# A two-layer fp32 encoder on one Trainium2 core: inner results of w_down's seven-product pairs added to X by adding DMAs, one such pair also in layer 0's last chunk, layer 1's attention steps sooner

## The chip, the cores and the metric

The kernel runs on one core of one Trainium2 chip. The metric is the device time of one execution in microseconds (us); lower is better. The median of three runs of the kernel before is 2045.56 us (2045.43 to 2046.12). One execution was profiled, and every time below that is not a run's time is read from that execution.

## The reference, cut to what matters

Sequence 256, model width 2048, two layers, everything in fp32. Layer 0 mixes tokens with a gated MLP, layer 1 with grouped-query attention (12 query heads, 4 key heads, head width 128, per-head norms and a rotary table). Both layers also attend into 256 memory tokens, and both end in a SwiGLU feed-forward part of width 5632.

```python
def gqa_axial_attention(qkv, g_q, g_k, cos, sin):
    ...
    def block(qi):
        s = jnp.einsum('bqhgd,bkhd->bhgqk', qi, k).astype(jnp.float32) * scale
        p = jax.nn.softmax(s, axis=-1).astype(v.dtype)
        return jnp.einsum('bhgqk,bkhd->bqhgd', p, v)
...
def swiglu(h, w_gate_up, w_down):
    gate, up = jnp.split(h @ w_gate_up, 2, axis=-1)
    return (jax.nn.silu(gate) * up) @ w_down
...
    for l in range(DEPTH):
        ...
        x = x + jnp.concatenate([tok_out, mem_out], axis=-1) @ w_out[l]
        x = x + swiglu(rms_norm(x, g_ffn[l]), w_gate_up[l], w_down[l])
```

## The kernel before

**Numbers.** Every fp32 operand is split into a high part (`whi`, a cast on ScalarE, L254) and a remainder (`wlo`, a subtraction on VectorE, L255), and each product is three TensorE matmuls (L198 to L200: high by high, low by high, high by low). X, the running sum of the layers, lies in SBUF as tiles `x_t_j`: t is one of two halves of 128 tokens, j one of four blocks of 512 columns.

**The feed-forward part.** The 5632 features are cut into eleven blocks of 512 and those into three chunks: blocks 0 to 3, 4 to 7 and 8 to 10. For each chunk a `Pair` per block makes gate and up, and then two `Pair`s (jj = 0 and 1) multiply by w_down, each for two of the four column blocks of X, and add into X. A `Pair` goes through pairs of 128 rows of the weight. A pair of rows that is listed as quick takes the step `seven`: seven products of sums instead of eight plain ones, 21 matmuls instead of 24, for which VectorE first makes sums of weights (L347 to L350, into the tile `T`, split like the others: `wlo<-T`) and sums of activations. The other rows take the step `eight`. Four PSUM banks named `m` collect the inner products of the quick steps, and four named `acc` the outer products and all of the plain steps.

After a Pair's last quick step `inner()` reads the `m` banks: ScalarE copies one to a tile e (L397), and VectorE makes v, f, v again and y from the others (L398 to L401). Where the Pair adds into X, the four tiles e, f, v and y are then added to their X tiles by four VectorE instructions (L405), put off by 1 to 4 ticks through `later`. The four tiles have one buffer each. After the Pair's last plain step `outer(t)` adds the `acc` banks to the same X tiles (L413), which sets those banks free for the next Pair.

In w_down the quick rows are two per Pair in chunks 0 and 1 of both layers and one in the last chunk of layer 1; the last chunk of layer 0 has none.

**Attention in layer 1.** For each of three groups of four heads (c = 0, 1, 2) a `linear` makes the queries and `attend` queues seven steps with `later`, by a clock that `linear` moves on once for each 12 matmuls and a Pair a few times for each step: `queries` turns them (heads_T), `scores` multiplies two heads by the keys and starts the softmax (on VectorE a maximum, L481, a reciprocal, L488, and a scaling, L490; on ScalarE the exponentials, L485), `turn` turns the probabilities by TensorE (L500), `weigh` multiplies by the values. `scores`, `turn` and `weigh` come twice, for two heads each, one tick apart. After the third group three more linears follow: the queries of the memory attention, and the keys and the values made of the memory. `head_norm` normalises such keys and queries straight from the `acc` banks (on VectorE in L431), which sets the banks free. With four `acc` banks, two for each linear, the values' linear can't begin before the norm of the memory's queries has been made.

**What sets the order.** The order in which the program is written out gives priorities, and a scheduler that simulates the engines' times then fixes the order of the instructions on each engine. On the chip each engine takes its instructions strictly in that order. The weights come by DMAs that SyncE issues into four `raw` buffers; `whi` and `wlo` have three buffers each. GpSimd's queue (POOL) issues few DMAs: tables, and the memory's rows (L551).

Of the kernel before, what the change touches and what calls it, by code (L numbers as in the profile page):

```python
# [13 lines left out]
ALU = mybir.AluOpType  # L14
# [39 lines left out]
def encoder(ctx: ExitStack, tc: tile.TileContext, x, mem, g_mix, g_ffn, w_in_a, g_v_a, w_spatial, b_spatial,  # L54
            w_in_b, g_q_b, g_k_b, g_mem, w_mem_kv, g_mq, g_mk, w_out, w_gate_up, w_down, rope_c, rope_s, out):
    nc = tc.nc
# [14 lines left out]
    def nm(s):  # L71
        uid[0] += 1
        return f"{s}_{uid[0]}"

    def big(dt=F32, shape=None):
        return room["p"].tile(shape or [P, NB], dt, tag="a", name=nm("a"))
# [4 lines left out]
    def misc():  # L81
        return psm.tile([P, NB], F32, tag="m", name=nm("m"))

    def v4(a):
        return a.rearrange("p (c n) -> p c n", n=P)
# [10 lines left out]
    def later(delay, fn):  # L96
        queue.append((clock[0] + delay, len(queue), fn))
# [39 lines left out]
    def gslice(kind, l):  # L137
        return gcol[kind][:, 16 * l:16 * l + 16]
# [7 lines left out]
    ghead, rope_t = {}, {}  # L146
# [41 lines left out]
    def split(src, shape):  # L188

        hi = big(F32R, shape)  # L190
        lo = big(F32R, shape)
        nc.scalar.copy(hi, src)  # L192
        nc.vector.tensor_tensor(lo, src, hi.bitcast(F32), ALU.subtract)  # L193
        return hi, lo
# [7 lines left out]
    def transpose4(src, dst):  # L202
        for c in range(4):
            nc.tensor.transpose(dst[:, c * P:(c + 1) * P], src[:, c * P:(c + 1) * P], ident)  # L204
# [85 lines left out]
    def linear(parts, w, n0, units=kd, nk=KD):  # L290
        return Linear(parts, w, n0, nk).run(units)
# [18 lines left out]
    class Pair:  # L310
# [82 lines left out]
        def inner(self):  # L393

            b, o = self.bank, self.into
            e, v, f, y = [room["p"].tile([P, NB], F32, tag=f"e{i}", name=nm("e"), bufs=1) for i in range(4)]
            nc.scalar.copy(e, b[1])  # L397
            nc.vector.tensor_tensor(v, b[6], e, ALU.subtract)  # L398
            nc.vector.tensor_tensor(f, b[5], v, ALU.add)
            nc.vector.tensor_tensor(v, b[7], v, ALU.add)  # L400
            nc.vector.tensor_tensor(y, b[7], f, ALU.add)  # L401
            if o:
                for (t, n), x, op in (((0, 0), e, ALU.add), ((0, 1), f, ALU.add), ((1, 0), v, ALU.subtract),
                                      ((1, 1), y, ALU.add)):
                    later(1 + 2 * t + n, lambda o=o[t][n], x=x, op=op: nc.vector.tensor_tensor(o, o, x, op))  # L405
            self.out = o or [[e, f], [v, y]]

        def outer(self, t):
# [190 lines left out]
    def residual_turns(j, norm, g, parts):  # L599
        add_residual(None, j, norm, g, parts)  # L600
# [3 lines left out]
    norm = Norm()  # L604
    for l in range(DEPTH):
# [4 lines left out]
        if l == 0:  # L610
            w = w_in_a[0]
            v = [[None] * 3 for _ in range(NT)]
# [72 lines left out]
            acc = lin.acc  # L685
# [4 lines left out]
            for c in range(3):  # L690
                if c:
                    acc = linear(hT, w, TOK + c * NB)
# [11 lines left out]
            for c in range(3):  # L704
                acc = linear(hT, w, c * NB)
# [5 lines left out]
        else:  # L711
            w = w_in_b[0]
            own = {}
            load_tables(1)
            m.prep(20, 2)
            acc = linear(hT, w, TOK)
# [6 lines left out]
            own["v"] = scaled(linear(hT, w, TOK + MEMW), norm.r)  # L723
            for c in range(3):
                acc = linear(hT, w, c * NB)
                attend(head_norm(acc, norm.r, ghead["q"], True), (7, 8, 11, 13), lambda: own["k"], lambda: own["v"],
                       lambda h, c=c: (4 * c + h) // 3, 4 * c, cat)
            m.attend(linear(hT, w, TOK + 2 * MEMW), norm.r, cat)
            m.keys()
# [3 lines left out]
        norm = Norm()  # L733
# [25 lines left out]
        next_norm = Norm()  # L759
        for chunk in (range(0, 4), range(4, 8), range(8, 11)):  # L760
            aT, aS, half = Parts(), {}, {}
            quick = [2 * f + 1 for f in chunk[:2 if chunk[-1] < 10 else l]]

            def turn_a(a, t, f, aT=aT, aS=aS, half=half, quick=quick):
                tp = misc()
                transpose4(a, tp)
                hi, lo = split(v4(tp), [P, 4, P])
                for i in range(4):
                    aT.put(4 * f + i, t, hi[:, i, :], lo[:, i, :])
                i = 2 * f + 1  # L770
                if i in quick:
                    half[i, t] = big(F32, [P, 2, P])
                    nc.scalar.copy(half[i, t], v4(tp)[:, 2:4])
                    if t == NT - 1:
                        aS[i] = activation_sums(half[i, 0], half[i, 1])

            pairs = {}
            for f in chunk:
                order, some = ((3, 4, 5, 0, 6, 1, 7, 2), 2) if f == 0 else ((0, 3, 1, 4, 2, 5, 6, 7), 3)
                pairs[f] = Pair(hF, sums, w_gate_up[l], f * NB, DFF + f * NB, order, fast[:some])  # L780
            for f, g in pairs.items():
                g.run(pairs.get(f + 1))
                for t in range(NT):
                    a = kp.tile([P, NB], F32, tag="sg", name=nm("sg"), bufs=2)
                    nc.scalar.activation(a, g.out[t][0], AF.Silu, scale=norm.r[t])
                    nc.vector.scalar_tensor_tensor(a, g.out[t][1], norm.r[t], a, ALU.mult, ALU.mult)
                    later(3 + t if f == chunk[-1] else 12 + t, lambda a=a, t=t, f=f: turn_a(a, t, f))
            last = chunk[-1] == 10
            every = [2 * f + c for f in chunk for c in range(2)]
            slow = [i for i in every if i not in quick]  # L790
            pairs = []
            for jj in range(2):
                order = list(slow)
                for n, i in enumerate(quick):
                    order.insert(2 * n + (0 if jj and not last else 2), i)
                into = [[X[t][2 * jj + n] for n in range(2)] for t in range(NT)]
                pairs.append(Pair(aT, aS, w_down[l], 2 * jj * NB, (2 * jj + 1) * NB, order, quick, into))
            for jj, g in enumerate(pairs):
                g.run(None if jj else pairs[1])
                for j in (2 * jj, 2 * jj + 1):  # L800
                    if last and l < DEPTH - 1:
                        residual_turns(j, next_norm, gslice("mix", l + 1), hT)
                    elif last:
                        for t in range(NT):
                            parts = 2 if j == 3 and t == NT - 1 else 1
                            for i in range(parts):
                                cs = slice(i * NB // parts, (i + 1) * NB // parts)
                                eng = nc.scalar if i else nc.sync
                                eng.dma_start(out[0, t * P:(t + 1) * P, j * NB + cs.start:j * NB + cs.stop],
                                              X[t][j][:, cs])  # L810
        norm = next_norm
# [36 lines left out]
```

## Time and profile before

| | before |
|---|---|
| median of three runs | 2045.56 us |
| profiled execution | 2045.77 us |
| its span in the profile | 2044.0 us |
| mean granted TensorE clock | 0.999 |
| TensorE matmul (PE) busy | 2028.7 us, 99% |
| VectorE (DVE) busy | 1604.7 us, 79% |
| ScalarE (ACT) busy | 1095.1 us, 54% |
| GpSimd (POOL) busy | 49.1 us, 2% |
| DMA queues of SyncE, share of 16 engines | 56.4% |

The span runs from the first to the last instruction that the profile shows; the profiled execution took 1.77 us more than it. A busy share is an average over the whole span. Matmuls are pipelined, so the times of single matmuls in the rows overlap, and the pitch from start to start is what one costs.

### The profile page before, as it was taken

What the parts mean: (1) busy time and instruction counts of PE and PEld (TensorE: products, weight loads), DVE (VectorE), ACT (ScalarE), POOL (GpSimd) and SP (SyncE); (2) the same over time, 40 slices, a digit from 0 to 9 for tenths busy, and PEclk for the clock granted to TensorE, in tenths of its full rate; (3) what the DMA queues carried; (4) which work ended last, traced back from release to release, by engine and by line L of the source; (5) the groups of instructions that cost most, each with busy time, mean ns of one, the idle gap of its engine ahead of it and who ended that gap; (6) DMA issues with size and microseconds to landing.
All of it is one profiled execution on the core that took longest, in us unless ns stands there. A gap on an engine that the chain in (4) does not pass through costs nothing.

```text
span 2044.0 us, 24691 instructions
## 1 busy us (share of the span) xinstructions
PE 2028.7 (99%) x9298; PEld 1679.5 (82%) x9298; DVE 1604.7 (79%) x1862; ACT 1095.1 (54%) x1389; POOL 49.1 (2%) x80
## 2 busy tenths in 40 slices
PE   8999999999999999999999999999999999999999
PEld 6888888888888888888888888888888888888887
DVE  5575557998888988887666876589979899798976
ACT  7765455455444554445556665555544455444552
POOL 2010000000000000000010100000000000000000
PEclk9999999999999999999999999999999999999999
DMA  9754554655656556566556434655666555665554
GB/s 330 249 177 159 187 187 148 227 168 203 208 190 220 169 201 208 200 215 209 188 190 212 157 124 142 206 179 172 205 206 211 200 176 195 206 216 196 181 197 138
DMA packets 202432, 396.08 MB, mean 194 GB/s; under 512 B 11068, under 2 KB 11432, under 8 KB 202312
## 3 DMA queue, kind: packets, MB, share of 16 engines
q1 hardware_dynamic: 198800, 385.79, 56.4%
q0 software_dynamic: 2048, 6.42, 1.0%
q10 hardware_dynamic: 1464, 2.28, 0.3%
q8 instruction: 73, 1.20, 0.2%
q14 instruction: 47, 0.39, 0.1%
HBM read 390.26 MB, written 4.19 MB: 193 GB/s over the span
## 4 chain that ended last, share of the span: by engine, by line
PE 94%; DVE 3%; DMA 1%; issue 1%; ACT 1%; SPq 0%; DVEq 0%; ACTq 0%
PE acc L200 27%; PE acc L198 27%; PE acc L199 27%; PE m L200 4%; PE m L198 4%; PE m L199 4%; PE m L204 2%; DVE wlo L255 1%; DMA raw<-in_w_gate_up 1%; ACT whi L254 0%; PE m L500 0%; DMA x<-in_x 0%; DMA raw<-in_w_down 0%; PE m L643 0%; DVE x L413 0%
## 5 line engine op out<-in xcount | busy, mean ns | idle before, releaser
L255 DVE TENSOR_TENSOR wlo<-raw,whi 128x2048 fp32r<-128x2048 f32 (+2 forms) x465 | 836.4, 1822 | 227.0 <-ACT whi L254 224.8
L254 ACT CAST whi<-raw 128x2048 fp32r<-128x2048 f32 (+2 forms) x465 | 700.9, 1539 | 584.6 <-PE acc L199 513.3
L198 PE MATMUL acc<-whi,h 128*128 128x512 f32 x1440 | 563.6, 392 | 0.8 <-ACT whi L254 0.8
L199 PE MATMUL acc<-whi,h 128*128 128x512 f32 x1440 | 562.6, 391 | 0.0
L200 PE MATMUL acc<-wlo,h 128*128 128x512 f32 x1440 | 523.8, 392 | 1.1 <-DVE wlo L255 1.1
L198 PE MATMUL acc<-whi,a 128*128 128x512 f32 x1062 | 415.4, 392 | 0.6 <-DVE a L431 0.6
L199 PE MATMUL acc<-whi,a 128*128 128x512 f32 x1062 | 414.9, 391 | 0.0
L200 PE MATMUL acc<-wlo,a 128*128 128x512 f32 x1062 | 398.8, 391 | 0.1
L200 PEld LDWEIGHTS acc<-wlo,h 128*128 128x128 f32 x1440 | 270.6, 188 | 56.9 <-DVE wlo L255 1.9
L198 PEld LDWEIGHTS acc<-whi,h 128*128 128x128 f32 x1440 | 270.7, 188 | 55.4 <-ACT whi L254 1.2
L199 PEld LDWEIGHTS acc<-whi,h 128*128 128x128 f32 x1440 | 270.6, 188 | 55.0
L200 PEld LDWEIGHTS acc<-wlo,a 128*128 128x128 f32 x1062 | 199.7, 188 | 41.5 <-DVE wlo L255 0.5
L198 PEld LDWEIGHTS acc<-whi,a 128*128 128x128 f32 x1062 | 199.9, 188 | 41.3 <-DVE a L431 0.8
L199 PEld LDWEIGHTS acc<-whi,a 128*128 128x128 f32 x1062 | 199.9, 188 | 40.5
L254 ACT CAST whi<-T 128x1536 fp32r<-128x1536 f32 x82 | 121.4, 1481 | 143.3 <-PE acc L199 104.1
L255 DVE TENSOR_TENSOR wlo<-T,whi 128x1536 fp32r<-128x1536 f32 x82 | 143.5, 1750 | 38.8 <-ACT whi L254 38.8
L198 PE MATMUL m<-whi,a 128*128 128x512 f32 x264 | 104.2, 395 | 0.7 <-ACT whi L254 0.7
L199 PE MATMUL m<-whi,a 128*128 128x512 f32 x264 | 102.8, 390 | 0.0
L347 DVE TENSOR_TENSOR raw<-raw 128x512 f32<-128x512 f32 x82 | 56.1, 684 | 56.4 <-DMA raw<-in_w_gate_up 54.3
L200 PE MATMUL m<-wlo,a 128*128 128x512 f32 x264 | 89.6, 389 | 0.0
L192 ACT CAST a<-m 128x512 fp32r<-128x512 f32 x80 | 46.3, 586 | 50.7 <-PE m L204 32.6
L193 DVE TENSOR_TENSOR a<-m,a 128x512 fp32r<-128x512 f32 x80 | 54.0, 683 | 17.5 <-ACT a L192 17.5
(126 smaller groups left out, 1469.0 us busy)
## 6 DMA issues: line engine op xcount, KB each, us to landing
raw<-in_w_gate_up SPq DMA_DIRECT2D x352, 512.0 KB, 4.7
raw<-in_w_down SPq DMA_DIRECT2D x176, 512.0 KB, 5.2
raw<-in_w_out SPq DMA_DIRECT2D x32, 1024.0 KB, 5.1
raw<-in_w_in_a SPq DMA_DIRECT2D x24, 1024.0 KB, 5.3
raw<-in_w_in_b SPq DMA_DIRECT2D x24, 1024.0 KB, 5.2
raw<-in_w_mem_kv SPq DMA_DIRECT2D x16, 1024.0 KB, 5.2
raw<-in_w_in_a SPq DMA_DIRECT2D x7, 512.0 KB, 6.1
x<-in_x SPq DMA_DIRECT2D x8, 256.0 KB, 5.7
```

Source lines behind the costliest of these rows:

```text
L192: nc.scalar.copy(hi, src)
L193: nc.vector.tensor_tensor(lo, src, hi.bitcast(F32), ALU.subtract)
L198: nc.tensor.matmul(out, lhsT=a[0], rhs=b[0], start=start, stop=False)
L199: nc.tensor.matmul(out, lhsT=a[1], rhs=b[0], start=False, stop=False)
L200: nc.tensor.matmul(out, lhsT=a[0], rhs=b[1], start=False, stop=stop)
L204: nc.tensor.transpose(dst[:, c * P:(c + 1) * P], src[:, c * P:(c + 1) * P], ident)
L254: nc.scalar.copy(hi[:, cut], raw[:, cut])
L255: nc.vector.tensor_tensor(lo[:, cut], raw[:, cut], hi[:, cut].bitcast(F32), ALU.subtract)
L347: nc.vector.tensor_tensor(raw[:, 0], raw[:, 0], raw[:, 1], ALU.add)
```

## The change

Three edits. In `inner()`, where a Pair adds into X, v is now made with the opposite sign (one instruction of another kind in place of L400), and e, f, v and y are added to X by four DMAs that GpSimd issues at once and that add to what lies at their destination; the four VectorE additions go. In layer 0's last chunk the first block's second pair of rows becomes quick for both w_down Pairs, as it is in layer 1 already. And layer 1's attention steps are put off by 5, 6, 10 and 13 ticks instead of 7, 8, 11 and 13.

```diff
             nc.vector.tensor_tensor(f, b[5], v, ALU.add)
-            nc.vector.tensor_tensor(v, b[7], v, ALU.add)
+            if o:
+                nc.vector.scalar_tensor_tensor(v, b[7], -1.0, v, ALU.mult, ALU.subtract)
+            else:
+                nc.vector.tensor_tensor(v, b[7], v, ALU.add)
             nc.vector.tensor_tensor(y, b[7], f, ALU.add)
             if o:
-                for (t, n), x, op in (((0, 0), e, ALU.add), ((0, 1), f, ALU.add), ((1, 0), v, ALU.subtract),
-                                      ((1, 1), y, ALU.add)):
-                    later(1 + 2 * t + n, lambda o=o[t][n], x=x, op=op: nc.vector.tensor_tensor(o, o, x, op))
+                for (t, n), x in (((0, 0), e), ((0, 1), f), ((1, 0), v), ((1, 1), y)):
+                    nc.gpsimd.dma_start(o[t][n], x, accum_op=ALU.add)
...
-                attend(head_norm(acc, norm.r, ghead["q"], True), (7, 8, 11, 13), lambda: own["k"], lambda: own["v"],
+                attend(head_norm(acc, norm.r, ghead["q"], True), (5, 6, 10, 13), lambda: own["k"], lambda: own["v"],
...
-            quick = [2 * f + 1 for f in chunk[:2 if chunk[-1] < 10 else l]]
+            quick = [2 * f + 1 for f in chunk[:2 if chunk[-1] < 10 else 1]]
```

Counted over the whole program, TensorE has 30 fewer matmuls into `acc` banks and 24 more into `m` banks. VectorE loses 40 additions of L405; for two more quick steps it gains 8 sums of weights, 2 splits of `T`, 8 instructions of `inner()` and the sums of activations (four of 128x128 and one split). ScalarE gains 2 splits of `T`, 2 copies and a few small ones. GpSimd gains 48 DMAs of 256 KB. In the kernel after, L401 and L404 are what L400 and L401 were, the adding DMA is L407, and lines from there on are two higher (outer's addition is L415, the turning of probabilities L502).

The order moves at three places. The first is on VectorE where layer 0's second chunk goes from the Pair jj = 0 to jj = 1 of w_down. The tiles e_1011, e_1012 and e_1013 are v, f and y; the x tiles are X; acc_978 to acc_981 are the outer banks; raw_1036, T_1037 and the wlo tiles belong to weights of the next steps. Before:

```order
L401 TENSOR_TENSOR e_1013_6112<-m_1000_6034,e_1012_6111 128x512
L405 TENSOR_TENSOR x_0_1_90<-x_0_1_90,e_1012_6111 128x512
L255 TENSOR_TENSOR wlo_1028_6232<-T_1021_6187,whi_1027_6231 128x1536 [waits PE_49,Activation_49]
L348 TENSOR_TENSOR T_1037_6266<-raw_1036_6263 128x512 [waits DVE_49]
L405 TENSOR_TENSOR x_1_0_93<-x_1_0_93,e_1011_6110 128x512 [waits DVE_49]
L405 TENSOR_TENSOR x_1_1_94<-x_1_1_94,e_1013_6112 128x512 [waits DVE_49]
L413 TENSOR_TENSOR x_0_0_89<-acc_978_5923,x_0_0_89 128x512 [waits PE_49]
L413 TENSOR_TENSOR x_0_1_90<-acc_979_5930,x_0_1_90 128x512 [waits DVE_49,PE_49]
L349 TENSOR_TENSOR T_1037_6266<-T_1037_6266,raw_1036_6263 128x512 [waits DVE_49]
L350 TENSOR_TENSOR T_1037_6266<-T_1037_6266,raw_1036_6263 128x512
L413 TENSOR_TENSOR x_1_0_93<-acc_980_5937,x_1_0_93 128x512 [waits DVE_49,PE_49]
L413 TENSOR_TENSOR x_1_1_94<-acc_981_5944,x_1_1_94 128x512 [waits DVE_49,PE_49]
```

After:

```order
L401 SCALAR_TENSOR_TENSOR e_1011_6110<-m_1000_6034,e_1011_6110 128x512 [waits DVE_49]
L404 TENSOR_TENSOR e_1013_6112<-m_1000_6034,e_1012_6111 128x512
L347 TENSOR_TENSOR raw_1036_6263<-raw_1036_6263 128x512 [waits DMAHW2_49,DMAHW1_49]
L255 TENSOR_TENSOR wlo_1028_6232<-T_1021_6187,whi_1027_6231 128x1536 [waits PE_49,Activation_49]
L348 TENSOR_TENSOR T_1037_6266<-raw_1036_6263 128x512 [waits DVE_49]
L415 TENSOR_TENSOR x_0_0_89<-acc_978_5923,x_0_0_89 128x512 [waits DMASW0_49,PE_49]
L415 TENSOR_TENSOR x_0_1_90<-acc_979_5930,x_0_1_90 128x512 [waits DMASW1_49,PE_49]
L349 TENSOR_TENSOR T_1037_6266<-T_1037_6266,raw_1036_6263 128x512 [waits DVE_49]
L350 TENSOR_TENSOR T_1037_6266<-T_1037_6266,raw_1036_6263 128x512
L415 TENSOR_TENSOR x_1_0_93<-acc_980_5937,x_1_0_93 128x512 [waits DMASW2_49,PE_49]
L415 TENSOR_TENSOR x_1_1_94<-acc_981_5944,x_1_1_94 128x512 [waits DMASW3_49,PE_49]
L255 TENSOR_TENSOR wlo_1039_6272<-raw_1024_6224,whi_1038_6271 128x2048 [waits DMAHW7_49,DMAHW0_49,Activation_49]
```

The four additions of f, v, y (and e, earlier) are gone, the additions of the banks have moved up, and each of these now waits for one of GpSimd's DMAs (DMASW0 to DMASW3); the split wlo_1039 follows on them in both.

The second place is on TensorE a little later there. m_1029 to m_1032 and acc_1033 to acc_1040 are banks of jj = 1; whi_1038 with wlo_1039, and whi_1042 and whi_1044, are split weights of its first steps. Before:

```order
L199 MATMUL acc_1035_6259<-whi_1038_6271,a_854_5214 128x512
L198 MATMUL acc_1040_6293<-whi_1038_6271,a_853_5213 128x512 [waits DVE_49]
L199 MATMUL acc_1040_6293<-whi_1038_6271,a_854_5214 128x512
L198 MATMUL m_1029_6235<-whi_1042_6303,a_904_5507 128x512 [waits Activation_49]
L199 MATMUL m_1029_6235<-whi_1042_6303,a_905_5508 128x512
L198 MATMUL m_1030_6239<-whi_1042_6303,a_915_5548 128x512
L199 MATMUL m_1030_6239<-whi_1042_6303,a_916_5549 128x512
L198 MATMUL m_1031_6243<-whi_1044_6307,a_915_5548 128x512 [waits Activation_49]
L199 MATMUL m_1031_6243<-whi_1044_6307,a_916_5549 128x512
L198 MATMUL m_1032_6247<-whi_1044_6307,a_915_5548 128x512
L199 MATMUL m_1032_6247<-whi_1044_6307,a_916_5549 128x512
L200 MATMUL acc_1033_6251<-wlo_1039_6272,a_846_5183 128x512 [waits DVE_49]
```

After:

```order
L199 MATMUL acc_1035_6259<-whi_1038_6271,a_854_5214 128x512
L198 MATMUL acc_1040_6293<-whi_1038_6271,a_853_5213 128x512 [waits DVE_49]
L199 MATMUL acc_1040_6293<-whi_1038_6271,a_854_5214 128x512
L200 MATMUL acc_1033_6251<-wlo_1039_6272,a_846_5183 128x512 [waits DVE_49]
L198 MATMUL acc_1033_6251<-whi_1038_6271,a_846_5183 128x512
L199 MATMUL acc_1033_6251<-whi_1038_6271,a_847_5184 128x512
L200 MATMUL acc_1033_6251<-wlo_1039_6272,a_846_5183 128x512
L200 MATMUL acc_1034_6255<-wlo_1039_6272,a_846_5183 128x512
```

The products with wlo_1039 now come ahead of those with whi_1042 and whi_1044.

The third place is on TensorE in layer 1, third group of heads. m_1582 holds scores of the group's last head, a_1557 the probabilities of its first, and acc_1627 is a bank of the memory's values. Before:

```order
L198 MATMUL m_1582_9488<-a_1339_8272,a_1550_9355 128x256 [waits PE_49]
L199 MATMUL m_1582_9488<-a_1339_8272,a_1552_9357 128x256
L200 MATMUL m_1582_9488<-a_1341_8274,a_1550_9355 128x256
L198 MATMUL m_1582_9488<-a_1339_8272,a_1550_9355 128x256
L199 MATMUL m_1582_9488<-a_1339_8272,a_1552_9357 128x256
L200 MATMUL m_1582_9488<-a_1341_8274,a_1550_9355 128x256
L500 MATMUL m_1590_9537<-ident_82,a_1557_9397 128x128 [waits DVE_49,Activation_49]
L500 MATMUL m_1590_9537<-ident_82,a_1557_9397 128x128
L500 MATMUL m_1590_9537<-ident_82,a_1557_9397 128x128 [waits DVE_49]
L500 MATMUL m_1590_9537<-ident_82,a_1557_9397 128x128
L198 MATMUL acc_1627_9732<-whi_1630_9736,a_1364_8435 128x512 [waits DVE_49]
L199 MATMUL acc_1627_9732<-whi_1630_9736,a_1365_8436 128x512
```

After, where m_1597 holds the scores of the last head, a_1581 the probabilities of the first and acc_1609 and acc_1610 banks of the memory's keys:

```order
L199 MATMUL acc_1610_9543<-whi_1645_9734,a_1506_9048 128x512
L200 MATMUL acc_1610_9543<-wlo_1646_9735,a_1505_9047 128x512
L198 MATMUL acc_1609_9542<-whi_1645_9734,a_1491_8966 128x512
L199 MATMUL acc_1609_9542<-whi_1645_9734,a_1492_8967 128x512
L200 MATMUL acc_1609_9542<-wlo_1646_9735,a_1491_8966 128x512
L198 MATMUL acc_1609_9542<-whi_1645_9734,a_1491_8966 128x512
L199 MATMUL acc_1609_9542<-whi_1645_9734,a_1492_8967 128x512
L502 MATMUL m_1614_9576<-ident_82,a_1581_9424 128x128 [waits DVE_49,Activation_49]
L502 MATMUL m_1614_9576<-ident_82,a_1581_9424 128x128
L502 MATMUL m_1614_9576<-ident_82,a_1581_9424 128x128 [waits DVE_49]
L502 MATMUL m_1614_9576<-ident_82,a_1581_9424 128x128
L200 MATMUL acc_1609_9542<-wlo_1646_9735,a_1491_8966 128x512
```

Before, the probabilities are turned right behind the last scores, and the values' products come next. After, 17 products of the memory's keys stand between the last scores (m_1597) and the turning, of which the last seven are shown, and the rest of that linear follows on it.

## Rows read from the trace of the kernel before

**Rows 1.** The page: busy time by engine, and the chain that ended last.
```profile
PE 2028.7 (99%) x9298; PEld 1679.5 (82%) x9298; DVE 1604.7 (79%) x1862; ACT 1095.1 (54%) x1389; POOL 49.1 (2%) x80
PE 94%; DVE 3%; DMA 1%; issue 1%; ACT 1%; SPq 0%; DVEq 0%; ACTq 0%
```

**Rows 2.** Waits of TensorE: line, what for, us in total, times, longest us.
```profile
PE m L500 <- DVE a L490: 2.6, 1, 2.6
PE acc L200 <- DVE wlo L255: 1.1, 1, 1.1
PE m L198 <- ACT whi L254: 0.7, 4, 0.2
```

**Rows 3.** The chain that ended last, near 721 us: start, us, what.
```profile
721.10 0.68 PE m L200 x3
```

**Rows 4.** TensorE's timeline, third head group: start, us, instruction, [idle before, releaser].
```profile
1205.55 0.28 PE L199 MATMUL m<-a,a 128*128 128x256 f32 x1
1205.67 0.28 PE L200 MATMUL m<-a,a 128*128 128x256 f32 x1
1208.58 0.63 PE L500 MATMUL m<-ident,a 128*128 128x128 f32 x4 [2.63 <-DVE a L490]
1209.79 0.79 PE L198 MATMUL acc<-whi,a 128*128 128x512 f32 x1 [0.58 <-DVE a L431]
...
1212.94 0.44 PE L199 MATMUL acc<-whi,a 128*128 128x512 f32 x1
1213.22 0.39 PE L200 MATMUL acc<-wlo,a 128*128 128x512 f32 x1
```

**Rows 5.** Windows there: busy us of PE, PEld, DVE, ACT, POOL, clock, DMA share, GB/s.
```profile
1209.79:1212.90 3.11, 3.11 (x7) 2.48 (x8) 2.75 (x12) 1.02 (x4) 0.45 (x1) 0.50 0.59 228
```

**Rows 6.** VectorE's timeline at the same place.
```profile
1205.36 0.68 DVE L481 TENSOR_REDUCE s<-m 128x2 f32<-128x512 f32 x1
...
1208.09 0.61 DVE L490 TENSOR_SCALAR a<-a,s 128x256 f32<-128x256 f32 x2
1208.61 2.15 DVE L431 SCALAR_TENSOR_TENSOR a<-acc,s,a 128x128 f32<-128x128 f32 x8
```

**Rows 7.** VectorE's timeline, layer 0's second chunk, from jj = 0 to jj = 1.
```profile
788.35 0.68 DVE L400 TENSOR_TENSOR e<-m,e 128x512 f32<-128x512 f32 x1
788.95 0.68 DVE L401 TENSOR_TENSOR e<-m,e 128x512 f32<-128x512 f32 x1
...
790.14 1.75 DVE L255 TENSOR_TENSOR wlo<-T,whi 128x1536 fp32r<-128x1536 f32 x1
...
797.22 4.48 DVE L255 TENSOR_TENSOR wlo<-raw,whi 128x2048 fp32r<-128x2048 f32 x2
```

**Rows 8.** TensorE's timeline just behind it.
```profile
798.99 0.45 PE L198 MATMUL m<-whi,a 128*128 128x512 f32 x1
...
799.73 0.40 PE L199 MATMUL m<-whi,a 128*128 128x512 f32 x1
800.32 0.50 PE L198 MATMUL m<-whi,a 128*128 128x512 f32 x1 [0.19 <-ACT whi L254]
```

**Rows 9.** The same place in layer 1's second chunk.
```profile
1813.45 0.50 PE L198 MATMUL m<-whi,a 128*128 128x512 f32 x1 [0.18 <-ACT whi L254]
```

**Rows 10.** GpSimd's DMAs from L551, from 1000 to 1300 us, and their landing.
```profile
L551 POOL DMA_DIRECT2D a<-memT x8: 536/554/615, 1059.8 to 1130.4; - x8
DMA to landing us min/median/max: 3.0/3.7/4.4
```

**Rows 11.** Landing of L551's DMAs over the whole span (also those of the start).
```profile
DMA to landing us min/median/max: 3.0/4.8/10.9
```

**Rows 12.** Windows, columns as in rows 5: L551's second stretch, then the last chunks of layers 0 and 1.
```profile
1055.00:1135.00 80.00, 80.00 (x373) 66.70 (x372) 59.00 (x111) 49.06 (x109) 10.03 (x14) 1.00 0.65 210
970.00:1036.00 66.00, 66.00 (x308) 54.68 (x307) 40.08 (x48) 36.86 (x71) 3.01 (x6) 1.00 0.60 188
1955.00:2035.00 80.00, 80.00 (x362) 66.25 (x361) 62.80 (x59) 34.73 (x26) 0.00 (x0) 1.00 0.49 158
```

## The prediction

> **What bounds the kernel now.** I read the page first. TensorE is busy 99% of the span and makes 94% of the chain that ended last [rows 1]. So two things alone can move the time: TensorE's own work, and the few places where it stands still or runs slowly. The pitch of its work is in the chain: three 128x512 matmuls take 0.68 us, 0.227 us each [rows 3].
>
> Then I read what TensorE waits for. Besides the start, the longest wait is one of 2.6 us at L500 for VectorE's scaling of the softmax (L490); the others that matter are single waits of 0.2 to 1.1 us for split weights [rows 2]. The timeline at the long wait shows more than the wait. The last score matmul starts at 1205.67, the turning at 1208.58, the next linear at 1209.79 after a second wait for L431, and from there the eighth matmul starts at 1212.94, at a mean pitch of 0.45 us; the next one follows 0.28 behind it, and then the pitch is back [rows 4]. In the slow stretch the granted clock is 0.50, so 1.2 instead of 2.4 GHz, right behind the idle time [rows 5]. Between 1205.67 and 1213.22 lie 7.55 us. The work in them is one score matmul and four turnings at 0.12 (the pitch of the two score rows; I take it for the turnings too) and eight wide matmuls at 0.227: 0.60 + 1.82 = 2.42 us. The place costs **5.1 us**: about 3.5 us of standing still and 1.6 us of slow matmuls.
>
> **The change, part by part.**
>
> *One more quick pair of rows.* Layer 0's last chunk takes one pair of rows by seven products in two Pairs: 2 x 3 = 6 matmuls fewer, 6 x 0.227 = **-1.36 us**, since TensorE is busy throughout that chunk (66.00 of 66.00 us) [rows 12]. The new work of VectorE there: eight sums and eight instructions of `inner()` at a pitch of 0.60, two splits of T at 1.75 [rows 7], and five small instructions of the activation sums at no more than 0.60 each, together about 16 us. VectorE is busy 40.08 of 66 us there, so the idle 26 us hide it. Layer 1's last chunk has this structure already, with VectorE busy 62.80 of 80 us and TensorE 80.00 of 80.00 [rows 12]. The lower bound is no loss; the upper is one wait like the longest for a split weight, 1.1 us [rows 2], in each of the two Pairs, 2.2 us. The nearest row is layer 1's own, with no wait; I put 0.3 us in the sum for a new small wait or two like the 0.2 us ones of L198 [rows 2].
>
> *Attention sooner.* The first head's probabilities in the third group are turned at 1208.58. Behind that head's scores come the 15 matmuls of the other scores at 0.12, so its scores ended about 1203.9: the softmax needed 4.7 us and the order gave it 1.8. From the maximum (L481 at 1205.36) to the end of the scaling (1208.70) are 3.3 us of that, the rest was VectorE's delay in taking up the maximum [rows 6]. In the new order six products of the memory's keys, 18 score matmuls and 17 more products stand between these scores and the turning: 23 x 0.227 + 18 x 0.12 = 7.4 us, 2.7 more than was needed. So the wait should go. The second wait, for L431, which frees the banks of the memory's queries for the values' linear, came because VectorE reached it behind the scaling (1208.09). It does so in the new order too, but behind the third head's scaling, and seven more products of the keys' linear and three turnings stand ahead of the values' linear; from L431's start to the first free bank it is 1.2 us (1208.61 to 1209.79 [rows 4, 6]), one turning covers 0.5, and so at most 0.7 us can stay if the third head comes just in time. If TensorE isn't idle, the slow clock has no cause. The bounds are 0 and 5.1 us; I take **-5.0 us**, because the margin is over half of the old delay, and leave 0.1 of those 0.7. The other two groups move in the same way; TensorE had no wait there worth a row in the view, so they give nothing.
>
> *Adding DMAs.* Forty additions of 0.60 us leave VectorE, 24 us. As VectorE is not the bound this is worth only the waits that they caused. At the passage from jj = 0 to jj = 1 VectorE is busy without a gap [rows 7], and 10 us behind it TensorE waits for a split: between 799.73 and 800.32 lie 0.59 us instead of 0.227, a loss of 0.36; layer 1 has its twin at 1813.45, with a wait of the same size, 0.18 for 0.19 [rows 8, 9]. In the new order the products with wlo_1039 fill that place, since VectorE comes to this split sooner. I count **-0.7 us** (bounds 0 and 0.7, and if the longest wait for a split, 1.1 us [rows 2], went too, -1.8).
>
> Against that stands the new wait: the additions of the outer banks wait until the DMAs have landed. GpSimd is busy 2% [rows 1], so issuing them (0.54 to 0.62 us each [rows 10]) delays nobody. How much time has a DMA? y is made 0.60 us sooner than before, at 788.95 instead of 789.55 (its own split ahead is unchanged, L347 now stands behind). Behind it VectorE has L347 (0.60), the split of T (1.67), L348, two outer additions, L349, L350 and the addition of x_1_0 (seven at 0.60 with L347, and the split: 5.9 us) before it needs y's DMA at about 794.8. It would then be at wlo_1039 at 795.4, where before it was at 797.22 [rows 7]. TensorE wants that split at 798.99, where the products with whi_1042 start in the old order [rows 8], and a split of that size takes 2.28 us (half of the 4.48 us of two, with what they overlap). So it may start at 796.7: a DMA that lands within 795.4 - 0.6 - 788.95 = 5.9 us costs VectorE nothing, and one within **7.1 us** costs TensorE nothing. Behind VectorE's wait stand this split and the next ones, on which TensorE lives.
>
> What does one take? The trace has no adding DMA. The nearest are GpSimd's other DMAs of 256 KB: 3.0 to 4.4 us, median 3.7 [rows 10], in a stretch with a DMA share of 0.65, more than the 0.49 and 0.60 of the last chunks [rows 12]. Below that it won't be. Above, an addition that moves everything twice can't be worse than two of the slowest one after the other, 8.8 us, unless the queue is as full as at the kernel's start, where the slowest took 10.9 [rows 11]. I take about 5.5, between one and two medians: no loss. The second Pairs (jj = 1) have more time, since a whole linear's worth of plain steps lies between.
>
> The Trainium skill has a rule that speaks against this: "Collectives: The Full Stack", section "The bandwidth ceiling: the fold count and why AG ≠ RS ≠ AR", says that an add done by the DMA engines reads two sources through one ring and so runs at about half the rate of a copy (32.35 against 62.28 GB/s there). With the line of "DMA: Bandwidth & Descriptors", section "Anatomy of one DMA — SWDGE (gpsimd) path", 2.0 us and the bytes at 436 GB/s, my estimate is 2.6 us for 256 KB and 3.2 with the moving part doubled, and the sum would be the same; but the shortest row here is 3.0 us and the median 3.7, so the page's line is too short for this kernel and the doubling is better weighed on rows. That is the second rival.
>
> *The sum.* -1.36 - 5.0 - 0.7 + 0.3 = -6.8 us. The profiled execution took 2045.77 us (span 2044.0 and 1.77 around it), so 2039.0; the median of the runs is 0.2 below that execution, and I forecast **2038.8 us**, 0.33% faster. 0.2%, 4.1 us, is about what a measurement of this kernel can tell from no change.
>
> **The rivals.**
>
> *First: the attention wait stays in part.* For it speaks that four softmaxes go through one VectorE in a row (3.3 us each in the rows, overlapping) and that the second pair of heads follows the first closely; against it the margin of 2.7 us. If half of the standing still remained, 1.75 us, the slow clock behind it would too, 1.6 us: 3.35 of the 5.0 us stay and the time is 2042.2 us, within 0.2%.
>
> *Second, on the other side: the adding DMAs land late.* Four are issued close together, each reading X as well as its tile, beside the weights' stream. The place is the four passages from jj = 0 to jj = 1 (chunks 0 and 1 of both layers), the price 4 us for each microsecond beyond 7.1. At 8.8 us it is 4 x 1.7 = 6.8, and the time 2045.6, no change; at 10.9 us 15.2, and 2054 us. It makes the kernel slower by over 0.2% (2049.7) from 9.8 us on. Against it speaks that no such DMA took over 4.4 us away from the start [rows 10]. The halved rate of the page named above would lead here.
>
> *Third: layer 0's last chunk.* If its quick step makes TensorE wait 1.1 us in each Pair, the upper bound above, the time is 2038.8 + 2.2 - 0.3 = 2040.7.
>
> **How the numbers follow.** The forecast has 55%: all three parts must come out. The first rival has 15%, the second 20% (half of it beyond 9.8 us), the third 10%. The forecast and about a third of the third rival, which comes with other small losses, end faster by over 0.2% (below 2041.5): 58%. The first, half of the second and most of what is left of the third end within 0.2%: 29%. Slower: 13%. The lower end is the sum without the 0.3, with the whole 5.1 and the 1.1 us wait gone too: -1.36 - 5.1 - 1.8 = -8.3 from 2045.56, **2037.3**. The upper end takes in the second rival up to two slow DMAs in a row, 2045.6, and some of its rest: **2046**. The likeliest case alone runs from 2037.3 to 2040.7.
>
> **What would show it.** In TensorE's waits the row of L500 (now L502) for 2.6 us is gone, and no stretch near 1205 us has a clock of 0.5. TensorE has six 128x512 matmuls fewer. The adding DMAs' median landing is 4 to 7 us, and VectorE's idle time before L415 that a DMA ended is under 1 us in all. I am wrong if that idle time is several us at each passage, if L502 still waits, or if TensorE waits for splits in layer 0's last chunk.

## The result, and the profile after

The change made the kernel slower: 2055.82 us in the median of four runs (2055.26 to 2057.39) against 2045.49 for the kernel before on the same chip (2044.51 to 2046.12), a ratio of 1.0049 (95% interval 1.0037 to 1.0061). That is the other side of the forecast, and outside its range.

The page of the kernel after: busy time, GpSimd's DMA queue (packets, MB, share of 16 engines), and its new issues (KB each, median us to landing):

```profile
PE 2028.2 (99%) x9292; PEld 1677.1 (82%) x9292; DVE 1597.7 (78%) x1845; ACT 1100.5 (54%) x1396; POOL 91.6 (4%) x128
...
q0 software_dynamic: 8960, 19.01, 4.5%
...
x<-e POOLq DMA_DIRECT2D x48, 256.0 KB, 7.6
```

TensorE does six matmuls fewer than in [rows 1] and is as busy, in a span that is 9.8 us longer. The adding DMAs land after 7.6 us in the median, not after 5.5. TensorE's waits, columns as in [rows 2]:

```profile
PE acc L200 <- DVE wlo L255: 13.8, 11, 1.8
...
PE acc L198 <- DVE x L415: 0.6, 2, 0.4
PE m L198 <- ACT whi L254: 0.4, 2, 0.2
```

Two things are to be seen. The wait of 2.6 us for the softmax is gone; nothing stands in the list for L502. And the waits for a split weight, one of 1.1 us before, are eleven with 13.8 us. The stretch of the third head group has no idle time and the full clock now (windows, columns as in [rows 5]):

```profile
1195.00:1225.00 30.00, 30.00 (x181) 26.42 (x180) 21.55 (x46) 20.05 (x54) 1.84 (x2) 1.00 0.42 141
```

The new waits have two kinds of places. TensorE's timeline shows the first of each kind, in layer 0's first chunk and behind it:

```profile
545.43 0.40 PE L199 MATMUL acc<-whi,a 128*128 128x512 f32 x1
547.29 0.50 PE L200 MATMUL acc<-wlo,a 128*128 128x512 f32 x1 [1.46 <-DVE wlo L255]
...
589.36 0.39 PE L199 MATMUL acc<-whi,h 128*128 128x512 f32 x1
591.17 0.50 PE L200 MATMUL acc<-wlo,h 128*128 128x512 f32 x1 [1.43 <-DVE wlo L255]
```

From 545.43 to 547.29 is 1.86 us where 0.23 is the pitch, from 589.36 to 591.17 1.81. The first lies at the passage from jj = 0 to jj = 1, the second at the start of the next chunk's gate and up. Counted in this way over all steps longer than 0.25 us beyond the pitch, the four passages of the first kind cost 2.0, 1.3, 1.6 and 1.6 us, 6.6 in all with rounding, and the four of the second kind 1.6, 1.6, 2.6 and 2.2, 8.0 in all. One more step of 0.6, at 781.96, lies 22 us ahead of the second passage's and is of neither kind. Layer 0's last chunk has none.

**The first kind: the bank additions wait.** VectorE's timeline at the first passage:

```profile
534.62 0.68 DVE L404 TENSOR_TENSOR e<-m,e 128x512 f32<-128x512 f32 x1
...
539.29 0.68 DVE L415 TENSOR_TENSOR x<-acc,x 128x512 f32<-128x512 f32 x1
542.64 0.69 DVE L415 TENSOR_TENSOR x<-acc,x 128x512 f32<-128x512 f32 x1 [2.67 <-PE acc L199]
544.35 0.69 DVE L415 TENSOR_TENSOR x<-acc,x 128x512 f32<-128x512 f32 x1 [1.01 <-PE acc L199]
544.96 4.48 DVE L255 TENSOR_TENSOR wlo<-raw,whi 128x2048 fp32r<-128x2048 f32 x2
```

y is ready at 535.3, the addition to its X tile starts at 544.35, and the split behind it, which before began at 543.12 by the same timeline, at 544.96. The bracket names TensorE, but in the kernel before the same two bank additions start at 541.92 and 542.52 without a wait, so the products are done by about then; what ended the two waits are the DMAs of v and y, issued at 535.00 and 535.83. One line's landing in a window that holds just these two:

```profile
DMA to landing us min/median/max: 7.6/7.8/8.1
```

535.00 + 7.6 and 535.83 + 8.1 are 542.6, the end of the first wait, and 543.9, 0.4 us ahead of the second's. At the other three passages the profile names the DMA itself, and the addition for y starts 0.1 us behind its landing; VectorE stands idle for these additions for 3.7, 2.8, 4.1 and 3.4 us in the four passages.

**The second kind: the weights come late.** After the Pair jj = 1 its four DMAs run beside the loads of the next chunk's first weights. VectorE's timeline there:

```profile
575.12 0.69 DVE L347 TENSOR_TENSOR raw<-raw 128x512 f32<-128x512 f32 x1 [4.22 <-DMA raw<-in_w_gate_up]
...
577.78 2.29 DVE L255 TENSOR_TENSOR wlo<-raw,whi 128x2048 fp32r<-128x2048 f32 x1
...
585.22 0.69 DVE L347 TENSOR_TENSOR raw<-raw 128x512 f32<-128x512 f32 x1 [2.29 <-DMA raw<-in_w_gate_up]
...
588.83 4.48 DVE L255 TENSOR_TENSOR wlo<-raw,whi 128x2048 fp32r<-128x2048 f32 x2
```

The load of this chunk's second weight tile took 11.7 us here and 7.1 in the kernel before, by the landing of L357 in a window that holds it alone, after and before:

```profile
DMA to landing us min/median/max: 11.7/11.7/11.7
```

```profile
DMA to landing us min/median/max: 7.1/7.1/7.1
```

The third tile's load runs beside the same DMAs, and the chain to TensorE's wait starts from it; its two halves, after and before:

```profile
DMA to landing us min/median/max: 8.2/8.6/9.1
```

```profile
DMA to landing us min/median/max: 3.8/4.2/4.7
```

It is there at 575.0, so that its sums (L347) start at 575.12; the split at 577.78 ends at 580.07; only then is a `raw` buffer free for a load, which is issued at 580.09 (573.87 before; 2 us of the difference are left from the first passage) and lands at 585.1; so the next sums and the next split are late, and TensorE waits until 591.17.

### The profile page after: what moved, and what is told of

It reads as the page before. It is cut to its first block, busy times and chain, and to the rows that moved or that the text cites. A ratio compares the mean times of both kernels' runs of the same rounds, so it can differ in the third digit from the quotient of the medians.

```text
span 2053.8 us, 24822 instructions
## 1 busy us (share of the span) xinstructions
PE 2028.2 (99%) x9292; PEld 1677.1 (82%) x9292; DVE 1597.7 (78%) x1845; ACT 1100.5 (54%) x1396; POOL 91.6 (4%) x128
## 4 chain that ended last, share of the span: by engine, by line
PE 79%; issue 12%; DMA 4%; DVE 4%; ACT 1%; SPq 0%; POOL 0%; DVEq 0%; ACTq 0%; POOLq 0%
PE acc L200 22%; PE acc L198 22%; PE acc L199 22%; PE m L198 3%; PE m L200 3%; PE m L199 3%; DMA raw<-in_w_gate_up 3%; DVE wlo L255 2%; PE m L204 2%; ACT whi L254 1%; PE m L502 0%; DMA x<-e 0%; DMA x<-in_x 0%; DMA raw<-in_w_down 0%; DVE T L350 0%
## 5 line engine op out<-in xcount | busy, mean ns | idle before, releaser
L198 PE MATMUL acc<-whi,a 128*128 128x512 f32 x1052 | 411.2, 392 | 0.2 <-DVE x L415 0.2
L199 PE MATMUL acc<-whi,a 128*128 128x512 f32 x1052 | 410.3, 390 | 0.0
L198 PEld LDWEIGHTS acc<-whi,a 128*128 128x128 f32 x1052 | 197.6, 188 | 40.8 <-DVE x L415 1.1
L199 PEld LDWEIGHTS acc<-whi,a 128*128 128x128 f32 x1052 | 197.6, 188 | 39.9
L347 DVE TENSOR_TENSOR raw<-raw 128x512 f32<-128x512 f32 x84 | 57.6, 685 | 90.9 <-DMA raw<-in_w_gate_up 83.6
L198 PE MATMUL m<-whi,a 128*128 128x512 f32 x272 | 106.9, 393 | 0.4 <-ACT whi L254 0.4
L199 PE MATMUL m<-whi,a 128*128 128x512 f32 x272 | 105.9, 389 | 0.0
L407 POOL DMA_DIRECT2D x<-e x48 | 42.2, 967 | 1348.7 <-ACT e L397 1264.5
```

Of the source, the lines that this page charges most:

```text
L198: nc.tensor.matmul(out, lhsT=a[0], rhs=b[0], start=start, stop=False)
L199: nc.tensor.matmul(out, lhsT=a[1], rhs=b[0], start=False, stop=False)
L347: nc.vector.tensor_tensor(raw[:, 0], raw[:, 0], raw[:, 1], ALU.add)
L407: nc.gpsimd.dma_start(o[t][n], x, accum_op=ALU.add)
```

## The experiments

Theory A: the adding DMAs alone cost. Theory B, its rival: the new order of sums, splits and additions on VectorE costs, with DMAs or without.

| run | median us | ratio to before (95%) |
|---|---|---|
| the changed kernel | 2055.82 | 1.0037 to 1.0061 |
| e1_vector_adds | 2039.62 | 0.9965 to 0.9984 |
| e2_dma_only | 2060.98 | 1.0065 to 1.0093 |
| e3_attention_only | 2040.12 | 0.9967 to 0.9986 |
| e4_quick_only | 2043.93 | 0.9986 to 1.0003 |
| e5_dma_first_pair | 2044.88 | 0.9987 to 1.0005 |
| e6_dma_second_pair | 2054.05 | 1.0031 to 1.0056 |
| e7_plain_copies | 2038.28 | 0.9952 to 0.9979 |
| e9_gpsimd_adds | 2044.19 | 0.9986 to 1.0003 |
| e10_no_adds | 2037.41 | 0.9950 to 0.9975 |
| e11_half | 2038.98 | 0.9957 to 0.9981 |
| e12_other_half | 2040.94 | 0.9969 to 0.9987 |

The kernel before was between 2045.1 and 2045.5 beside these runs.

**The parts one by one.** The first run is the kernel before with the change's second and third edits and without the adding DMAs, so VectorE adds as before:

```diff
-                attend(head_norm(acc, norm.r, ghead["q"], True), (7, 8, 11, 13), lambda: own["k"], lambda: own["v"],
+                attend(head_norm(acc, norm.r, ghead["q"], True), (5, 6, 10, 13), lambda: own["k"], lambda: own["v"],
...
-            quick = [2 * f + 1 for f in chunk[:2 if chunk[-1] < 10 else l]]
+            quick = [2 * f + 1 for f in chunk[:2 if chunk[-1] < 10 else 1]]
```

The other three are the kernel before with one part of the change each.

> The changed kernel with the four additions back on VectorE (quick pair and sooner attention kept). Theory A (the adding DMAs alone cost: at the passage from jj = 0 to jj = 1 the bank additions wait for them, and after jj = 1 they delay the next chunk's weights): the 15 us of new TensorE gaps at the eight passages go, the gain of about 6 us stays, 2039 us. Theory B (the new order costs, with or without DMAs, because VectorE's sums and splits were moved): the gaps at the second kind of passage stay, some 2046 us.

> The kernel before with the adding DMAs alone. Theory A: the gaps of about 15 us come in full, less the two old waits of 0.5 us, and nothing is gained: 2060 us, with landings of 7 to 8 us in the median. Theory B gives the same 2060 us only if the order is the same; with other waits it would be nearer 2052.

> The kernel before with layer 1's attention steps sooner and nothing else. Both theories: the place near 1205 us gives back 5.0 to 5.2 us, 2040.4 us. If the gap only moves to another head group, 2043 or more.

> The kernel before with the quick pair of rows in layer 0's last chunk and nothing else (the inner results added by VectorE). Six matmuls of 0.227 us less: 2044.2 us. If VectorE's added 16 us aren't hidden there, 2045.5 or more.

All four came out within a microsecond of what theory A expects. The adding DMAs cost 16.2 us beside the other two parts (2055.82 - 2039.62) and 15.9 alone (2060.98 - 2045.1); the steps counted above, with the one at 781.96, come to 15.2. The attention part gives 5.0 us (2045.1 - 2040.12); its window, columns as in [rows 5]:

```profile
1200.00:1226.00 26.00, 26.00 (x142) 22.29 (x142) 21.01 (x48) 17.25 (x45) 1.84 (x2) 1.00 0.35 122
```

The quick pair gives 1.2, inside its interval's noise, and brings one new wait of TensorE in layer 0's last chunk (e4, behind 1027.65):

```profile
PE acc L198 <- DVE x L413: 0.3, 1, 0.3
```

The profile of e2 has the old wait as well as the new ones, PE's waits:

```profile
PE acc L200 <- DVE wlo L255: 11.6, 9, 1.8
...
PE m L502 <- DVE a L492: 2.6, 1, 2.6
```

**One kind of passage alone.** The DMAs add for one of the two Pairs; for the other VectorE does:

```diff
-                    nc.gpsimd.dma_start(o[t][n], x, accum_op=ALU.add)
+                    if not self.na:
+                        nc.gpsimd.dma_start(o[t][n], x, accum_op=ALU.add)
+                    else:
+                        later(1 + 2 * t + n, lambda o=o[t][n], x=x: nc.vector.tensor_tensor(o, o, x, ALU.add))
```

and with `self.na` for jj = 1.

> The changed kernel with adding DMAs for jj = 0 only; jj = 1 adds on VectorE. If the two kinds of passage cost by themselves, the wait of the bank additions at the four passages from jj = 0 to jj = 1 stays (7.3 us of gaps in the changed kernel, 0.9 of which is there without DMAs), and the gaps at the next chunk's start go: 2039.6 + 6.4 = 2046. If the DMAs of one Pair are late because those of the other are still under way, it is under 2043.

> The changed kernel with adding DMAs for jj = 1 only. Crowding of the weights: the first gate and up weights of the next chunk land late (8 to 12 us instead of 4 to 7) and the gaps there, 8.0 us in four places, stay: 2039.6 + 8 = 2047.6. If only the wait of the bank additions costs, nothing is lost here, since these come 11 us behind y: 2040.

The first costs 5.3 us over e1 (2044.88 - 2039.62), a microsecond under the forecast by places. The second costs 14.4, far more than the 8.0 that I expected, and more than its share: the two make 19.7, not 16.2. The rows say why. The waits for splits between 500 and 2030 us are fewer, but longer (e6, waits of TensorE):

```profile
PE acc L200 <- DVE wlo L255: 10.1, 4, 3.4
```

so that the four places cost 2.0, 3.3, 2.4 and 3.6 us beyond the pitch, 11.2 in all with rounding. And behind three of them the granted clock falls to half, 1.2 of 2.4 GHz, which costs some 1.5 us each time (eight matmuls from 589.08 to 592.45, 3.4 us where the pitch makes 1.8; the profiled run is 0.9 us over the median). The timeline and windows of e6, at the first and the last of the four:

```profile
587.77 0.50 PE L200 MATMUL acc<-wlo,h 128*128 128x512 f32 x1 [1.80 <-DVE wlo L255]
...
589.08 0.63 PE L198 MATMUL acc<-whi,h 128*128 128x512 f32 x1
589.50 0.63 PE L199 MATMUL acc<-whi,h 128*128 128x512 f32 x1
...
1858.52 0.39 PE L199 MATMUL acc<-whi,h 128*128 128x512 f32 x1
1862.31 0.79 PE L200 MATMUL acc<-wlo,h 128*128 128x512 f32 x1 [3.40 <-DVE wlo L255]
1862.90 0.63 PE L198 MATMUL acc<-whi,h 128*128 128x512 f32 x1
1863.33 0.63 PE L199 MATMUL acc<-whi,h 128*128 128x512 f32 x1
```

```profile
589.00:592.00 3.00, 3.00 (x8) 2.32 (x8) 2.59 (x2) 0.00 (x0) 0.00 (x0) 0.50 0.98 347
1862.10:1865.00 2.90, 2.69 (x6) 2.15 (x7) 2.90 (x3) 0.00 (x0) 0.00 (x0) 0.51 0.55 165
```

Without the delays of the first kind, the DMAs of jj = 1 and the load of the next chunk's third weight tile start closer together here, and that load takes 10.5 to 11.4 us in layer 0's second chunk where it took 8.3 to 9.3 in the changed kernel; that this closeness is what makes the waits longer is a reading, no run takes it apart.

**The addition itself.** The DMAs copy instead of adding; X then holds e, f, v and y alone at that point.

```diff
-                    nc.gpsimd.dma_start(o[t][n], x, accum_op=ALU.add)
+                    nc.gpsimd.dma_start(o[t][n], x)
```

> The changed kernel with the 48 DMAs as plain copies of e, f, v and y over X, so that what X held is lost; the same bytes are written, by the same queue, with the same waits behind them. If the addition itself is dear (a second read for each byte), the landing falls from 7.6 us to 4 to 5 in the median and the time to 2041 to 2044. If any 256 KB from GpSimd's queue crowds the weights in this way, landing stays above 6.5 and the time above 2051.

This decides between the theories. The order of instructions on TensorE, VectorE and ScalarE is the same as in the changed kernel, the bytes written too, and the time is 2038.28, under the forecast of this study. The order costs nothing; what costs is that the DMA adds. An adding DMA also has more packets and a longer issue; the run takes these away together with the adding, so it doesn't tell by which of them the adding costs. The page of e7, GpSimd's queue and its landings:

```profile
q0 software_dynamic: 5888, 19.01, 2.6%
...
x<-e POOLq DMA_DIRECT2D x48, 256.0 KB, 6.2
```

A run without these DMAs (e10, below) has

```profile
q0 software_dynamic: 2048, 6.42, 1.1%
```

so the 48 copies take 1.5% of the DMA engines' span in 80 packets each, and the 48 additions 3.4% (4.5 less 1.1) in 144: an addition takes 2.3 times a copy's time. My second guess in that expectation was wrong: landing falls only to 6.2, not to 5, and yet the gaps go. The reason is in the slack: the copies of v and y at the first passage land after

```profile
DMA to landing us min/median/max: 6.0/6.2/6.4
```

6.0 and 6.4 us, between the 5.9 that cost VectorE nothing and the 7.1 that cost TensorE nothing; y's copies at the four passages take 6.0, 7.1, 5.9 and 6.9. TensorE's whole wait for splits in e7 is

```profile
PE acc L200 <- DVE wlo L255: 0.5, 1, 0.5
```

and the load of the next chunk's second weight tile takes 9.0 instead of 11.7 us:

```profile
DMA to landing us min/median/max: 9.0/9.0/9.0
```

The Trainium skill's page "Collectives: The Full Stack", section "The bandwidth ceiling: the fold count and why AG ≠ RS ≠ AR", puts the add of a collective at half of a copy's rate because it reads two sources; the share of 3.4 against 1.5% is near that, a factor of 2.3, while no run here shows the reason.

**GpSimd's own additions, and none.** One line each:

```diff
-                    nc.gpsimd.dma_start(o[t][n], x, accum_op=ALU.add)
+                    nc.gpsimd.tensor_tensor(o[t][n], o[t][n], x, ALU.add)
```

and, for e10, nothing in its place: X lacks e, f, v and y.

> The changed kernel with the four additions as GpSimd instructions instead of DMAs: VectorE is as free as in the changed kernel, no DMA is added. If the gaps come from the DMAs' transfers, they go, and since VectorE's freed time is worth little the time is that of the kernel with VectorE's additions, 2039 to 2040. If GpSimd's additions take over about 2 us each or hold up VectorE's own, 2043 or more.

> The changed kernel without any addition of the inner results (X lacks e, f, v and y): no DMA and no VectorE addition. It shows what VectorE's freed 24 us are worth at the most. If nearly nothing, because TensorE is the bound and the waits that they caused are two of 0.5 us, it is 2038.5 to 2039.5, within about 1 us of the kernel with VectorE's additions (2039.62) and of the plain copies (2038.28). If VectorE's work mattered more than I hold, 2036 or less.

Without any addition the kernel takes 2037.41: VectorE's freed 24 us are worth 2.2 us at the most (2039.62 - 2037.41), a little more than the 1 that I expected. Four steps of TensorE that e1 has and e10 lacks make 1.6 of it, counted beyond the pitch, with rounding: 0.4 at each of 522.88, 799.64 and 1806.81, and 0.5 at 1027.87 in layer 0's last chunk. GpSimd's additions lose 4.6 us against VectorE's (2044.19 - 2039.62). They take 1.3 to 3.8 us each, 1.6 in the median, and hold up VectorE's instructions with two inputs in SBUF; VectorE's timeline of e9 beside one that runs from 786.01 to 789.3, beside two that run from 790.51 to 794.57, and behind them, beside nothing:

```profile
788.05 1.78 DVE L347 TENSOR_TENSOR raw<-raw 128x512 f32<-128x512 f32 x1
...
793.34 1.78 DVE L348 TENSOR_TENSOR T<-raw 128x512 f32<-128x512 f32 x1
...
796.84 0.67 DVE L349 TENSOR_TENSOR T<-T,raw 128x512 f32<-128x512 f32 x1
```

The page "SBUF — State Buffer" of the Trainium skill, section "Who interferes with whom", states that such an instruction contends with one of GpSimd that reads SBUF; 1.78 against 0.67 us agree.

**Half of the traffic.** DMAs for e and f only (t = 0), VectorE for v and y; and the other way round.

```diff
-                    nc.gpsimd.dma_start(o[t][n], x, accum_op=ALU.add)
+                    if t == 0:
+                        nc.gpsimd.dma_start(o[t][n], x, accum_op=ALU.add)
+                    else:
+                        later(1 + 2 * t + n, lambda o=o[t][n], x=x: nc.vector.tensor_tensor(o, o, x, ALU.add))
```

> The changed kernel with e and f added by DMA and v and y by VectorE: half of the adding traffic, and the two that start first. If crowding by the DMAs' own time is the cause, the weights' loads are late by half as much, and since the slack at both passages is some 2 us most of the gaps go: 2039 to 2042. If it were enough that bank additions wait for any adding DMA, half of the 7.3 us at the first kind of passage stays and the time is 2043 to 2046.

> As the run with e and f by DMA, but the other half: v and y, which are ready last, by DMA, and e and f by VectorE. The traffic is the same. If the amount of adding traffic decides, landings are about 6.7 us and the time is 2039 to 2041. If it is decisive that v and y have only 5.9 us to VectorE's and 7.1 us to TensorE's next need, the first kind of passage costs as in the changed kernel (7 us in four places): 2045 to 2047.

Both are nearly free of the gaps, with 2038.98 and 2040.94: TensorE's waits for splits between 500 and 2030 us, 12.6 in the changed kernel, are 1.2 and 1.1. The first has landings of

```profile
x<-e POOLq DMA_DIRECT2D x24, 256.0 KB, 6.7
```

and the second, with the tiles that are ready last, of

```profile
x<-e POOLq DMA_DIRECT2D x24, 256.0 KB, 6.4
```

So among DMAs that add it is less which tile they add that decides than how many run at once: with two additions a Pair, v's and y's landings at the four passages (e12) are 5.4 to 7.5 us, about TensorE's slack; with four, y's are 8.1 to 9.0 and the weights are pushed past theirs. e5 has as many adding DMAs in all as e11, 24, but four at once, and is 5.9 us slower. The fastest versions that compute everything are e11, e1, e3 and e12, 2039.0 to 2040.9. Their intervals overlap, so the runs don't set them apart; they beat the kernel before by 4.3 to 6.4 us.

## Why the prediction was wrong

**The attention part was right**: -5.0 forecast, 5.0 measured alone, wait and slow clock gone together, and no new wait at L502 or L433 (the old L431).

**The quick pair was right in size**: -1.36 and 0.3 for new waits make -1.1, and 1.2 was measured, though the noise of that run would hide it. Alone it brings the one wait of 0.3 us; in the changed kernel layer 0's last chunk has no wait of TensorE. The third rival did not come.

**The two old waits**, -0.7, do go with VectorE's additions: e10 and e7 have no such step at these two places, e1 still has. In the changed kernel this is lost in the new gaps.

**The step that failed is the cost of the adding DMAs**, put at nothing because they would land after about 5.5 us and have 7.1. The slack was read rightly: landings of y of 8.1, 8.5, 8.9 and 9.0 us at the four passages would by 7.1 have cost 1.0 + 1.4 + 1.8 + 1.9 = 6.1 us, and these places cost 6.6 (2.0, 1.3, 1.6 and 1.6), while 5.9 to 7.1 us in e7 cost nothing. The landing was not: I took a value between the median and twice the median of L551's loads, 3.7 us. The plain copies of e7 take 6.2 us in the median, and v's and y's additions at the four passages 7.6 to 9.0, with 2.3 times the engines' time. The sign that I had named, several us of VectorE's idle time at each passage, is there: 2.8 to 4.1. L551's loads didn't have the engines to themselves: they came three, four and one together. The four that are issued from 1104.17 on, in the kernel before, have this landing:

```profile
DMA to landing us min/median/max: 3.0/3.7/4.4
```

The window there, and that of e7 where v's and y's copies landed after 6.4 and 6.0 us:

```profile
1104.00:1110.00 6.00, 6.00 (x28) 4.98 (x27) 5.76 (x15) 2.56 (x4) 2.38 (x5) 1.00 0.90 307
534.00:541.00 7.00, 7.00 (x32) 5.82 (x31) 5.51 (x8) 1.92 (x1) 1.07 (x2) 1.00 0.79 298
```

With a DMA share of 0.90 they landed sooner than the copies with 0.79, so neither the number at once nor the share accounts for the difference. L551 loads from DRAM, the copies go from SBUF to SBUF; whether that is the reason stays open. The upper bound, 8.8 us, was no bound either: y's last two landings are over it, and behind jj = 1 some take 10.3 and 10.5. The second rival described this place and its price, and the doubling behind it; I gave it 20%.

**What no step and no rival had** is the second kind of place. "The second Pairs (jj = 1) have more time" asked only who waits for these DMAs. Nobody had to: they took the DMA engines' time from the weights of the next chunk, whose loads have too little slack there, and this cost 8.0 us, more than the wait that I had worked out. With the rival's own price alone, 6 to 7 us, the time would have been 2045 to 2046, near the kernel before; with both, 14.6 us on 2038.8, it is 2053.4, and 2055.82 was measured. Of the rest, 0.6 is the step at 781.96; 1.8 us are not placed.

## What to carry to other kernels

Work that is moved to DMA queues from an engine that is not the bound buys little (here at most 2.2 us of 24) and can be paid in the bound's supply: count it as a load on the DMA engines beside the transfers that feed the bound (here 2.3 times a copy's time for an addition), and look for the place where those transfers have little slack, also where nothing waits for the new DMAs. A landing time that is read from other DMAs at another place may not hold: 3.7 us there was 6.2 for copies here. Half of the additions, two at once, cost nothing clear here, so the load can be tried in steps. Steps of a chain that is late (attention here) are worth moving when the chain's own time and the work now put ahead of it can be read from rows: that term came out to a tenth.

## What the runs showed of the hardware

An adding DMA of 256 KB lands in 3.3 us where little else runs (2.3 as a copy), in 7.6 us in the median here. GpSimd takes longer to issue it: 0.87 us in the median against 0.54. And waits of the same length have had two prices: behind one of 1.80 us in e6 (587.77) the granted clock was 0.50, with a pitch of 0.43 us for some 3 us, as behind the old attention wait [rows 4, 5], and behind one of 1.77 us in the changed kernel, at the same kind of place, it stayed at 1.00. The changed kernel's timeline and window there:

```profile
1864.60 0.50 PE L200 MATMUL acc<-wlo,h 128*128 128x512 f32 x1 [1.77 <-DVE wlo L255]
```

```profile
1864.40:1867.00 2.60, 2.40 (x11) 2.00 (x12) 2.60 (x3) 0.00 (x0) 0.00 (x0) 1.00 0.46 109
```

So the length of the wait alone doesn't say whether the clock falls; what does is not shown.
